# Other constants in the table of durations that orders the queues of a hybrid DeltaNet and window-attention layer

## The chip, the cores and the metric

The kernel runs on one core of one Trainium2 chip. The core has five instruction queues that matter here: TensorE (PE, its weight loads shown as PEld), VectorE (DVE), ScalarE (ACT), GpSimd (POOL) and SyncE (SP), which only issues DMAs. Each queue runs its instructions strictly in order; an instruction that waits holds up everything behind it on its queue. The metric is the device time of one execution, in microseconds. Before the change it is 1352.76 us, the median of three runs (1352.02 to 1355.77).

## The reference

One encoder layer: RMSNorm, one input projection, two groups of heads that read the same normalised rows, one output projection, and a residual. All is float32, with 2048 rows and a model width of 1024.

```python
h = rms_norm(x, norm_w[l])
proj = h @ w_in[l]
# A: 4 DeltaNet heads of 128, chunks of 64, forward and backward
qkv = jax.nn.silu(centred_depthwise_conv(concat([q, k, v]), conv_w))
t_inv = triangular_solve(eye + m, eye, lower=True, unit_diagonal=True)
u = t_inv @ (v * beta); w = t_inv @ (k * beta * exp(g))
# scan over chunks:
v_new = u_i - w_i @ state
o     = (q_i * exp(g_i)) @ state + a_i @ v_new
state = state * exp(g_last) + k_dec.T @ v_new
# B: 8 query heads of 64 over 2 key heads, |i-j| <= 128, a sink logit per head
p = exp(scores - mx); out = (p / (sum(p) + exp(sink - mx))) @ v
mix = concat([rms_norm(dn, w) * silu(dn_z), sw * silu(sw_z)])
x = x + mix @ w_out[l]
```

## The kernel before

**Two stages.** The function `phase_a` (up to some 800 us) splits the normalised x into a high and a low part (type float32r) and makes every product of the projection out of three matmuls of 512 columns: `proj_feat` (L186 to L188, tiles `pf_c` and `pf_z`, transposed results) and `proj_seq` (L197 to L199, `pq_q`). `conv_pair` (L212 to L246) takes a pair of channel blocks: it has ScalarE write the first tap into `acc` (L233) and VectorE add the four others straight from the PSUM tile `pf_c` (L237), and stores q and k into `kq_d`, v into `v_d`. A bank of `pf_c` comes free when the last L237 on it is done. `attend` treats one block of 128 query rows: scores `s` (L339 and L340), masked row maxima on VectorE (L341, one custom instruction per head, which writes `pr`), the exponentials on ScalarE (L346), the scaling of `pr` on GpSimd (L355), transposes of `pr` on TensorE (L360, `pt`), their split (L364 and L365, `ph` and `pl`) and the products with v.

**The DeltaNet stage.** `phase_b` has for each of four heads: `pre_front` (from L588), `pre_back` (from L671) and `scan` (from L750). `pre_front` runs over four groups of four chunks, in the order 1, 2, 0, 3: it loads `kq` (L604, 512 KB, two buffers) and `vt`, transposes them (L621 `tr`, L660 `trv`), forms the Gram matrices `gh` (L641), has VectorE scale them into `ma` (L650) and stores these to `m_d` in DRAM (L655). `pre_back` loads `L` from `m_d` and solves all chunks' triangular systems at once by 31 steps of two VectorE instructions each (L687 into `tm`, L691 into `X`), stores X (L692), loads it in spread form (`xc`, L740) and completes the inverse with 16 times four small matmuls (L703, `pza`, `pra`, `pzb`, `prb`). `scan` goes over 16 chunks in both directions: `pk` (L767), `r` on VectorE (L769), `py` (L776), `yk` and `y` on ScalarE (L781, L783), `po` (L778, L785, L794), the new state `S` on VectorE (L788) and the sums into `oacc` (L801 to L805). `post_rows` transposes `oacc` (L833, `tro`), loads the gate `zt` (L835), multiplies (L836) and stores to `mix_dn`. `out_half` is the output projection: its window-attention half (`pcs`) stands in the program behind the first `pre_front`, its DeltaNet half (`pcd`, L559 to L561, with loads L550 and L556 and the sum L562) at the end. Names carry the head, the direction or the group, and the chunk: `ma3_2_0` is head 3, group 2, direction 0.

**What sets the order.** The program is written head after head, but the queues aren't run in that order. `set_order` (from L875) takes all instructions, builds the graph of what must come before what (data, buffers that have to come free, PSUM banks), and gives each a duration from a table, `cost` (L1003), and each edge a lag: `LAG` between engines, `SAME` for a result that its own engine reads, and for a DMA the issue time (`cost` for SP) plus a time to land (`LAG["SP"]`, `move`, which is bytes / 300 and also occupies one common bus, and `late`). `plan` is a list scheduler: it picks for the engine that is free earliest the ready instruction of the highest rank. It is run forwards and backwards twelve times, each pass ranking by the times of the one before, and the order with the least end by its own reckoning is kept. The result is pinned: each instruction gets a dependency on its predecessor on its queue. So the table decides nothing but the order; no instruction, tile or buffer hangs on it.

Of the kernel before, what the change touches and what calls it, by code (L numbers as in the profile page):

```python
# [13 lines left out]
DRAM = bass.MemoryType.DRAM  # L14
# [860 lines left out]
def set_order(tc):  # L875
# [127 lines left out]
    def cost(i, eng):  # L1003
        o = aps(i.outs)
        m, ins = size(o[0]), aps(i.ins)
        if eng == "SP":
            return 500
        if eng == "PE":
            if i.is_transpose:
                return 110  # L1010
            if "float32r" in str(i.ins[0].dtype):
                return max(112, m / 2.4 + 14)
            return 2 * (max(m, size(ins[1]) if len(ins) > 1 else P, 40) / 1.2 + 5)
        scalars = sum(size(a) == 1 for a in ins)
        if eng == "Activation":
            return 60 + 0.86 * m + 85 * (scalars > 0) + 110 * (len(o) > 1)
        m = max([m] + [size(a) for a in ins])
        if eng == "DVE":
            if i.opcode == "Reciprocal":
                return 70 + 6.2 * m  # L1020
            if i.opcode == "TensorScalarPtr" and len(ins) - scalars < 2:
                return 60 + 0.6 * m
            return 70 + 1.04 * m + 55 * (scalars > 0) + 10 * (i.opcode == "ISA")
        if i.opcode == "TensorTensor":
            return 350 + 165 * min(m, 4) if m <= 16 else 180 + 2.1 * m
        return 150 + 1.02 * m

    total = len(succ)
    dur = [cost(i, e) for i, e in insts] + [0] * (total - n)
# [3 lines left out]
    for k in range(total):  # L1033
        if eng[k] == "SP":
            a = aps(insts[k][0].outs)[0]
            move[k] = a.ap[0][1] * size(a) * 4 / 300
            spread = [x.ap[0][0] == 0 for x in aps(insts[k][0].ins)]
# [178 lines left out]
```

## Time and profile before

| | before |
|---|---|
| median of 3 runs | 1352.76 us |
| the profiled execution, device time | 1354.61 us |
| its span in the trace | 1352.8 us |
| mean granted TensorE clock | 0.982 |
| GpSimd busy | 442.8 us |
| ScalarE busy | 684.2 us |
| transfers | 217.99 MB at a mean of 161 GB/s |

A profile is one execution. Its page gives the busy time of each engine, the span cut into slices, the transfers, the chain of work that ended last (followed back from the last instruction, at each step to what released it) and the costliest groups of instructions. A row of a group reads: line, engine, operation, out <- in by tile names, shape, count | busy us, mean ns of one | idle time of the engine ahead of them, and what ended most of it. A row of waits reads: engine, tile and line that waited <- what released it: us in all, number of waits, the longest. A row of the timeline reads: start, duration, engine, line, operation, tiles, and in brackets the idle time ahead of it and what ended it. Since matmuls overlap, a matmul's duration is longer than its share of the queue; starts tell how fast a row of them runs.

### The profile page before, as it was taken

How to read it: one execution, taken by the hardware profiler on the slowest of the kernel's cores; microseconds unless marked ns; L12 is line 12 of the kernel's file. 1: busy time of each engine (PE TensorE's matmuls, PEld its weight loads, DVE VectorE, ACT ScalarE, POOL GpSimd, SP SyncE). 2: the span in 40 equal slices, each digit the busy share in tenths (PEclk: the TensorE clock that was granted, in tenths of full speed). 3: DMA queues.
4: the chain of work that ended last, by engine and by line, in shares of the span. 5: the costliest groups of instructions: out<-in, count | busy, mean ns of one | idle time of the engine just before them, and what ended most of it. 6: DMA issues, size and time to landing. Idle time of an engine off the chain costs nothing.

```text
span 1352.8 us, 22281 instructions
## 1 busy us (share of the span) xinstructions
PE 1252.7 (93%) x7034; PEld 1052.7 (78%) x7034; DVE 938.7 (69%) x2362; ACT 684.2 (51%) x2009; POOL 442.8 (33%) x574
## 2 busy tenths in 40 slices
PE   5999989999999999999999997887898998997988
PEld 5998868888898987876788776776686786785766
DVE  4422577767878778888979767777779779755333
ACT  6321354425767777866645326664465644454200
POOL 2330062104666677864412114212521510300000
PEclk9999999999999999998999998997999999998999
DMA  8342254244522344412267537788786874646575
GB/s 282 113 135 94 72 161 156 74 129 137 176 74 87 118 143 121 148 32 79 95 223 215 175 113 231 223 230 250 231 245 182 251 189 146 192 129 195 165 247 187
DMA packets 238261, 217.99 MB, mean 161 GB/s; under 512 B 50368, under 2 KB 189376, under 8 KB 238144
## 3 DMA queue, kind: packets, MB, share of 16 engines
q1 hardware_dynamic: 238144, 216.58, 52.8%
q8 instruction: 56, 0.92, 0.3%
q14 instruction: 61, 0.50, 0.1%
HBM read 143.05 MB, written 73.47 MB: 160 GB/s over the span
## 4 chain that ended last, share of the span: by engine, by line
PE 63%; DVE 14%; DMA 9%; ACT 5%; POOL 4%; issue 4%; SPq 1%; POOLq 0%; DVEq 0%; ACTq 0%
PE pf_c L186 4%; PE pf_c L188 4%; PE pf_c L187 4%; PE pf_z L186 4%; PE pf_z L188 4%; PE pf_z L187 3%; PE pt L360 2%; PE pcd L560 2%; PE pcd L559 2%; DMA m_d<-ma 2%; PE pcd L561 2%; DVE acc L237 2%; DMA kq<-kq_d 2%; PE pq_q L197 2%; PE pq_q L199 2%
## 5 line engine op out<-in xcount | busy, mean ns | idle before, releaser
L186 PE MATMUL pf_c<-xhi,wh_c 128*128 128x512 f32 x384 | 151.2, 405 | 4.2 <-DVE acc L237 4.2
L237 DVE SCALAR_TENSOR_TENSOR acc<-pf_c,cw,acc 128x512 f32<-128x512 f32 (+1 forms) x192 | 140.0, 744 | 21.6 <-ACT acc L233 19.8
L187 PE MATMUL pf_c<-xlo,wh_c 128*128 128x512 f32 x384 | 149.8, 401 | 0.0
L188 PE MATMUL pf_c<-xhi,wl_c 128*128 128x512 f32 x384 | 149.4, 402 | 0.0
L355 POOL TENSOR_SCALAR pr<-pr,st 128x384 f32<-128x384 f32 (+1 forms) x128 | 85.3, 684 | 79.6 <-DVE st L353 38.4
L186 PE MATMUL pf_z<-xhi,wh_z 128*128 128x512 f32 x256 | 92.5, 404 | 1.4 <-DVE zo L210 1.4
L781 ACT ACTIVATE yk<-py,ck 128x128 f32<-128x128 f32 x120 | 43.9, 366 | 93.5 <-PE py L776 92.7
L187 PE MATMUL pf_z<-xlo,wh_z 128*128 128x512 f32 x256 | 91.0, 398 | 0.0
L188 PE MATMUL pf_z<-xhi,wl_z 128*128 128x512 f32 x256 | 90.7, 398 | 0.0
L346 ACT ACTIVATE pr<-pr,st 128x384 f32<-128x384 f32 (+1 forms) x128 | 76.3, 598 | 23.4 <-DVE st L345 21.3
L186 PEld LDWEIGHTS pf_c<-xhi,wh_c 128*128 128x128 f32 x384 | 73.0, 191 | 19.2 <-DVE acc L237 4.5
L188 PEld LDWEIGHTS pf_c<-xhi,wl_c 128*128 128x128 f32 x384 | 72.9, 190 | 15.7 <-issue 0.4
L187 PEld LDWEIGHTS pf_c<-xlo,wh_c 128*128 128x128 f32 x384 | 73.1, 190 | 14.2
L360 PE MATMUL pt<-ident,pr 128*128 128x128 f32 x368 | 73.3, 281 | 7.5 <-POOL pr L355 3.9
L341 DVE CUSTOM_DVE_ANT_0 pr<-s,mask,sink 128x384 f32<-128x384 f32 (+1 forms) x128 | 72.8, 593 | 10.1 <-PE s L340 4.7
L365 DVE TENSOR_TENSOR pl<-pt,ph 128x512 fp32r<-128x512 f32 x92 | 62.1, 683 | 20.6 <-ACT ph L364 16.8
L364 ACT ACTIVATE ph<-pt 128x512 fp32r<-128x512 f32 x92 | 53.6, 596 | 44.5 <-PE pt L360 38.3
L360 PEld LDWEIGHTS pt<-ident,pr 128*128 128x128 f32 x368 | 46.9, 142 | 26.6 <-POOL pr L355 10.6
L197 PE MATMUL pq_q<-wh_q,xhi 128*128 128x256 f32 x256 | 66.6, 287 | 0.1
L198 PE MATMUL pq_q<-wh_q,xlo 128*128 128x256 f32 x256 | 66.1, 285 | 0.0
L199 PE MATMUL pq_q<-wl_q,xhi 128*128 128x256 f32 x256 | 65.5, 286 | 0.0
L559 PE MATMUL pcs<-wohs,mhs 128*128 128x512 f32 x128 | 58.0, 453 | 7.6 <-ACT wohs L541 3.9
(250 smaller groups left out, 3668.2 us busy)
## 6 DMA issues: line engine op xcount, KB each, us to landing
m_d<-ma SPq DMA_DIRECT2D x32, 512.0 KB, 5.9
kqc<-kq_d SPq DMA_DIRECT2D x120, 128.0 KB, 3.4
ws_c<-wt SPq DMA_DIRECT2D x48, 256.0 KB, 3.7
xr<-x SPq DMA_DIRECT2D x16, 512.0 KB, 5.4
ws_z<-wt SPq DMA_DIRECT2D x32, 256.0 KB, 3.8
kq<-kq_d SPq DMA_DIRECT2D x16, 512.0 KB, 6.3
at<-m_d SPq DMA_DIRECT2D x128, 64.0 KB, 3.2
xrs<-x SPq DMA_DIRECT2D x32, 256.0 KB, 3.7
```

Source lines behind the costliest of these rows:

```text
L186: T.matmul(ps, hi[:, k, cs], xhi[b][:, k], start=(k == 0), stop=False)
L187: T.matmul(ps, hi[:, k, cs], xlo[b][:, k], start=False, stop=False)
L188: T.matmul(ps, lo[:, k, cs], xhi[b][:, k], start=False, stop=(k == KC - 1))
L197: T.matmul(ps[:, :n], xh, hi[:, k, :n], start=(k == 0), stop=False)
L198: T.matmul(ps[:, :n], xl, hi[:, k, :n], start=False, stop=False)
L199: T.matmul(ps[:, :n], xh, lo[:, k, :n], start=False, stop=(k == KC - 1))
L237: V.scalar_tensor_tensor(av, ps[:, lo:], cw[:, i, k : k + 1], av, ALU.mult, ALU.add)
L341: V.tensor_tensor_reduce(pr[j][:, :n], ps[:, :n], mask[:, lo * P : hi * P], 1.0, sink[:, hh : hh + 1], ALU.add, ALU.max, accum_out=mx[:, j ...
L346: A.activation(pr[j][:, :n], pr[j][:, :n], AF.Exp, bias=nm[:, j : j + 1], accum_out=den[:, j : j + 1])
L355: G.tensor_scalar(pr[j][:, :n], pr[j][:, :n], den[:, j : j + 1], 1.0, ALU.mult, ALU.mult)
L360: T.transpose(pt[:, j], pr[j][:, (kb - lo) * P : (kb - lo + 1) * P], ident)
L559: T.matmul(ps, mh[:, k], wh[:, k, ns], start=(k == 0), stop=False)
```

## The change

The table gets other constants, in four parts. For SP, the general lag of 2400 ns goes, an issue costs 520 or 670 ns instead of 500 (by the number of dimensions of its access pattern), and a new function `landing` gives each transfer its time to land: by size, with 1900 ns and 190 bytes per ns for loads, 1800 ns for what is written to DRAM at 450 or 190 bytes per ns, 1000 ns more for loads that read one row for many partitions and 1200 ns more for runs of under 64 elements. `move`, the common bus, stays. For TensorE, VectorE and ScalarE the fixed part of each duration grows by 3 to some 20 ns for most forms; operands that begin at a partition other than 0 get 115 ns more on VectorE and ScalarE (`off`). For GpSimd the fixed part grows by 60 to 70 ns. Nothing else in the kernel is changed.

```diff
-LAG = {"PE": 205, "DVE": 140, "Activation": 160, "Pool": 120, "SP": 2400}
+LAG = {"PE": 205, "DVE": 140, "Activation": 160, "Pool": 120, "SP": 0}
...
-            return 500
+            dims = max(sum(c > 1 for _, c in list(a.ap)[1:]) for a in (o[0], ins[0]))
+            return 520 if dims < 2 else 670
+        off = 115 * (o[0].ap[0][0] > 0 and o[0].offset // o[0].ap[0][0] % P > 0)
...
-                return max(112, m / 2.4 + 14)
+                return max(112, m / 2.4 + 18) + 5
...
-            return 70 + 1.04 * m + 55 * (scalars > 0) + 10 * (i.opcode == "ISA")
+            return 88 + 1.04 * m + 55 * (scalars > 0) + 10 * (i.opcode == "ISA") + off
...
-        return 150 + 1.02 * m
+        return 210 + 1.02 * m + 0.4 * off
+
+    def landing(i):
+        o, a = aps(i.outs)[0], aps(i.ins)[0]
+        n = o.ap[0][1] * size(o) * 4
+        if o.tensor.name in tiles and "DRAM" in str(tiles[o.tensor.name].space):
+            return 1800 + n / (450 if sum(c > 1 for _, c in o.ap) < 3 else 190)
+        run = min([c for t, c in list(a.ap) + list(o.ap) if t == 1] or [1])
+        return 1900 + n / 190 + 1000 * any(t == 0 for t, _ in a.ap) + 1200 * (run < 64)
...
-            late[k] = 2000 * any(spread)
-        lag = LAG[eng[k]] + move[k] + late[k] if k < n else 0
+            late[k] = landing(insts[k][0])
+        lag = LAG[eng[k]] + late[k] if k < n else 0
```

The orders of all five queues come out otherwise, with the same instructions in them. Three places:

On VectorE, in the first stage, where the first attention block's softmax (`pr0`, `st0`) meets the first convolutions (`acc4` and `acc5`, which empty the banks `pf_c`), stood before:

```order
L345 TENSOR_SCALAR st0_0_1496<-st0_0_1496 128x1
L349 TENSOR_TENSOR st0_0_1496<-sink_140,st0_0_1496 128x4
L341 ISA pr0_1_0_1562,st0_1_1566<-s0_4_1567,mask_130,sink_140 128x256
L341 ISA st0_1_1566 128x1
L281 TENSOR_TENSOR t1k3_1807<-t1k3_1807,rsk3_1813 128x128
L341 ISA pr0_1_1_1563,st0_1_1566<-s0_5_1573,mask_130,sink_140 128x256
L341 ISA st0_1_1566 128x1
L345 TENSOR_SCALAR st0_1_1566<-st0_1_1566 128x1
L237 SCALAR_TENSOR_TENSOR acc4_0_2046<-pf_c4_0_0_2050,cw_128,acc4_0_2046 128x512
L237 SCALAR_TENSOR_TENSOR acc5_0_2048<-pf_c5_0_0_2080,cw_128,acc5_0_2048 128x512
L237 SCALAR_TENSOR_TENSOR acc4_0_2046<-pf_c4_0_0_2050,cw_128,acc4_0_2046 128x512
L237 SCALAR_TENSOR_TENSOR acc5_0_2048<-pf_c5_0_0_2080,cw_128,acc5_0_2048 128x512
```

and now, from the rotary step `t1q1` on:

```order
L281 TENSOR_TENSOR t1q1_1460<-t1q1_1460,rsq1_1466 128x512
L300 TENSOR_TENSOR kd2_1445<-t1k2_1433,kd2_1445 128x2x128
L237 SCALAR_TENSOR_TENSOR acc4_0_2046<-pf_c4_0_0_2050,cw_128,acc4_0_2046 128x512
L237 SCALAR_TENSOR_TENSOR acc5_0_2048<-pf_c5_0_0_2080,cw_128,acc5_0_2048 128x512
L237 SCALAR_TENSOR_TENSOR acc4_0_2046<-pf_c4_0_0_2050,cw_128,acc4_0_2046 128x512
L237 SCALAR_TENSOR_TENSOR acc5_0_2048<-pf_c5_0_0_2080,cw_128,acc5_0_2048 128x512
L237 SCALAR_TENSOR_TENSOR acc4_0_2046<-pf_c4_0_0_2050,cw_128,acc4_0_2046 128x511
L237 SCALAR_TENSOR_TENSOR acc5_0_2048<-pf_c5_0_0_2080,cw_128,acc5_0_2048 128x511
L237 SCALAR_TENSOR_TENSOR acc4_0_2046<-pf_c4_0_0_2050,cw_128,acc4_0_2046 128x510
L237 SCALAR_TENSOR_TENSOR acc5_0_2048<-pf_c5_0_0_2080,cw_128,acc5_0_2048 128x510
L237 SCALAR_TENSOR_TENSOR acc4_0_2046<-pf_c4_0_1_2110,cw_128,acc4_0_2046 128x512
L178 TENSOR_TENSOR wl_c8_0_2412<-ws_c8_0_6_2425,wh_c8_0_2411 128x2x256
```

The eight L237 rows of the first bank pair, and the first of the next bank, have moved from behind the softmax rows of the heads 0 to 5 to a place ahead of all of them; the first L341 row (`pr0_0_0`) now stands two rows behind this piece.

On TensorE, in the DeltaNet stage, at head 2's `pre_front`, where the Gram matmuls `gh2_1_1` and `gh2_2_0` read `kq` of the groups 1 and 2 and `tr2_0_0` is the first to read the reloaded buffer of group 0, stood before:

```order
L641 MATMUL gh2_1_1_11260<-kq2_1_11205 128x256 x2
L794 MATMUL po0_0_12_10664<-y0_0_12_10669,at0_0_12_10655 128x128
L621 MATMUL tr2_2_1_11312<-ident_66,kq2_2_11285 128x128 x4
L776 MATMUL py0_1_12_10685<-r0_1_12_10683,tt0_0_9626 128x128
L767 MATMUL pk0_0_13_10749<-S0_0_12_10672,kqc0_0_13_10747 128x128
L660 MATMUL trv2_2_11355<-ident_66,vt2_2_11287 128x128 x4
L785 MATMUL po0_1_12_10686<-yk0_1_12_10689,ks0_0_8737 128x128
L833 MATMUL tro0_1_10723<-ident_66,oacc0_1_10321 128x128 x4
L641 MATMUL gh2_2_0_11329<-kq2_2_11285 128x256 x2
L621 MATMUL tr2_0_0_11377<-ident_66,kq2_0_11365 128x128 x4
```

and now, from the same first row, the first part of what lies between:

```order
L641 MATMUL gh2_1_1_11260<-kq2_1_11205 128x256 x2
L621 MATMUL tr2_2_1_11312<-ident_66,kq2_2_11285 128x128 x4
L778 MATMUL po0_0_12_10664<-S0_0_11_10628,kqc0_0_12_10657 128x128
L785 MATMUL po0_0_12_10664<-yk0_0_12_10667,ks0_3_8807 128x128
L778 MATMUL po0_1_12_10686<-S0_1_11_10650,kqc0_1_12_10679 128x128
L559 MATMUL pcs2_0_8986<-wohs_8867,mhs2_8980 128x512
L660 MATMUL trv2_2_11355<-ident_66,vt2_2_11287 128x128 x3
L794 MATMUL po0_0_12_10664<-y0_0_12_10669,at0_0_12_10655 128x128
L660 MATMUL trv2_2_11355<-ident_66,vt2_2_11287 128x128
L641 MATMUL gh2_2_0_11329<-kq2_2_11285 128x256 x2
L833 MATMUL tro0_1_10723<-ident_66,oacc0_1_10321 128x128
L560 MATMUL pcs2_0_8986<-wohs_8867,mls2_8979 128x512
```

Behind this piece follow two more rows of `tro0_1` and ten of the chunk product `pcs2_0`, and only then `tr2_0_0`. Twelve matmuls of `pcs2_0`, each 512 columns wide, now stand between `gh2_1_1` and `tr2_0_0`, and some scan rows (`py0_1_12`, `pk0_0_13`) have gone from there.

On VectorE, in the same stage, where head 2's solve (`tm2`, `X2`) runs beside head 1's scan (`r1`, `S1`, `oacc1`), the end of the solve and the first rows behind it read before:

```order
L691 TENSOR_TENSOR X2_12303<-X2_12303,tm2_30_12398 128x31
L769 SCALAR_TENSOR_TENSOR r1_1_12_12071<-pk1_1_12_12069,negc_5022,vs1_0_10052 128x128
L788 SCALAR_TENSOR_TENSOR S1_0_12_12060<-S1_0_11_12016,egt_5024,po1_0_12_12052 128x128
L632 RECIPROCAL ssk3_12586<-ssk3_12586 128x4
L633 TENSOR_TENSOR bp3_12588<-beta_4996,ssk3_12586 128x2x4
L804 SCALAR_TENSOR_TENSOR oacc1_3_11555<-po1_0_12_12052,egc_5026,oacc1_3_11555 128x128
L822 SCALAR_TENSOR_TENSOR sso1_1_12087<-sso1_1_12087 128x8
L562 TENSOR_TENSOR xrs8_0_9218<-xrs8_0_9218,pcs8_0_9220 128x512
L805 TENSOR_TENSOR oacc1_3_11555<-po1_0_12_12052,oacc1_3_11555 128x128
L650 SCALAR_TENSOR_TENSOR ma3_2_0_12680<-gh3_2_0_12717,bp3_12588,dc3_2_0_12677 128x256
L650 SCALAR_TENSOR_TENSOR ma3_2_1_12684<-gh3_2_0_12717,bp3_12588,dc3_2_1_12681 128x256
L650 SCALAR_TENSOR_TENSOR ma3_2_0_12680<-gh3_2_0_12717,bp3_12588,dc3_2_0_12677 128x256
```

and now, in the middle of the solve:

```order
L687 TENSOR_TENSOR tm2_11_12341<-L2_12302,X2_12303 128x240
L802 TENSOR_TENSOR oacc1_1_11709<-po1_0_7_11832,oacc1_1_11709 128x128
L691 TENSOR_TENSOR X2_12303<-X2_12303,tm2_11_12341 128x20x12
L788 SCALAR_TENSOR_TENSOR S1_1_7_11862<-S1_1_6_11818,egt_5024,po1_1_7_11854 128x128
L687 TENSOR_TENSOR tm2_12_12344<-L2_12302,X2_12303 128x247
L650 SCALAR_TENSOR_TENSOR ma3_2_0_12680<-gh3_2_0_12717,bp3_12588,dc3_2_0_12677 128x256
L691 TENSOR_TENSOR X2_12303<-X2_12303,tm2_12_12344 128x19x13
L769 SCALAR_TENSOR_TENSOR r1_1_8_11895<-pk1_1_8_11893,negc_5022,vs1_1_9892 128x128
L687 TENSOR_TENSOR tm2_13_12347<-L2_12302,X2_12303 128x252
```

The eight L650 rows of head 3's group 2 (`ma3_2`) stood behind the last solve step and now stand singly between its steps, from the twelfth on.

More of the change, by code (lines that the diff above doesn't have):

```diff
@@ L1019, in cost @@
             if i.opcode == "Reciprocal":
[L1020 removed]
+                return 80 + 6.2 * m
             if i.opcode == "TensorScalarPtr" and len(ins) - scalars < 2:
[L1022 to L1023 removed]
+                return 70 + 0.6 * m
+            return 88 + 1.04 * m + 55 * (scalars > 0) + 10 * (i.opcode == "ISA") + off
         if i.opcode == "TensorTensor":
[L1025 to L1026 removed]
+            return 420 + 165 * min(m, 4) if m <= 16 else 250 + 2.1 * m
+        return 210 + 1.02 * m + 0.4 * off
[6 more added lines that the diff above has]
+        return 1900 + n / 190 + 1000 * any(t == 0 for t, _ in a.ap) + 1200 * (run < 64)
     total = len(succ)
```

7 lines of the change are left out of this document (3 added, 4 removed).

## The prediction

> **What bounds the kernel now.** I read the page first, for the shares and for where TensorE is not full, and then the same stretch by stage.
>
> ```profile
> PE 1252.7 (93%) x7034; PEld 1052.7 (78%) x7034; DVE 938.7 (69%) x2362; ACT 684.2 (51%) x2009; POOL 442.8 (33%) x574
> ...
> PE 63%; DVE 14%; DMA 9%; ACT 5%; POOL 4%; issue 4%; SPq 1%; POOLq 0%; DVEq 0%; ACTq 0%
> ```
>
> TensorE is busy for 93% of the span and makes 63% of the chain that ended last; the other 37% of the chain are places where it stood and another engine or a transfer was late. No instruction is added or removed, so the change can only move those places. The windows (columns: stretch, length, then the busy time of PE, PEld, DVE, ACT and POOL, the granted clock, the DMA share, GB/s) tell where they are:
>
> ```profile
> 700.00:800.00 100.00, 98.46 (x440) 79.58 (x439) 81.65 (x165) 37.89 (x108) 15.34 (x15) 1.00 0.59 177
> 800.00:900.00 100.00, 82.38 (x521) 71.03 (x520) 66.93 (x179) 58.62 (x218) 30.88 (x24) 0.95 0.77 215
> 900.00:1000.00 100.00, 85.06 (x461) 70.05 (x462) 71.84 (x207) 53.48 (x224) 36.27 (x27) 0.90 0.80 240
> 1000.00:1100.00 100.00, 91.75 (x611) 77.81 (x610) 86.57 (x269) 58.34 (x241) 29.03 (x22) 1.00 0.72 211
> 1100.00:1200.00 100.00, 91.23 (x608) 77.92 (x607) 75.24 (x235) 44.86 (x162) 14.44 (x10) 1.00 0.60 168
> 1200.00:1300.00 100.00, 87.86 (x462) 71.29 (x461) 49.06 (x129) 34.63 (x121) 3.27 (x2) 0.97 0.59 185
> ```
>
> Up to 800 us TensorE is almost full. From 800 to 1300 it idles 61.7 us (the sum of 100 minus its busy time), and between 800 and 1000 its clock falls as well. That second stage, the DeltaNet heads, is where an order can win or lose most. How fast TensorE gets through a row of matmuls is read from starts, since its busy times overlap:
>
> ```profile
> 220.10 0.40 PE L186 MATMUL pf_c<-xhi,wh_c 128*128 128x512 f32 x1
> 220.34 0.39 PE L187 MATMUL pf_c<-xlo,wh_c 128*128 128x512 f32 x1
> ```
>
> and, for the 128-wide float32 ones,
>
> ```profile
> 1111.51 0.39 PE L767 MATMUL pk<-S,kqc 128*128 128x128 f32 x2
> 1111.73 0.39 PE L778 MATMUL po<-S,kqc 128*128 128x128 f32 x2
> ```
>
> A 512-wide matmul starts 0.24 us after the one before it (0.23 over a longer row), a 128-wide float32 one 0.22 us.
>
> **The change, place by place.** The new constants raise most engine durations by a few per cent alike, TensorE and VectorE by 3 to 4% on the 512-wide shapes, which by itself leaves an order as it is. What differs is GpSimd (60 to 70 ns more per operation) and the DMAs: a 512 KB load from a feature tensor is now taken to land later (1900 + 524288/190 = 4.7 us instead of 2400 + 524288/300 = 4.1), small loads and all stores sooner. I take the places where TensorE waited longest and look whether the new order changes what stands there.
>
> Place A, the first convolutions beside the first softmax:
>
> ```profile
> PE pf_c L186 <- DVE acc L237: 4.2, 1, 4.2
> ```
>
> What VectorE did just then, and the window around it:
>
> ```profile
> 177.35 1.22 DVE L281 TENSOR_TENSOR t1q<-t1q,rsq 128x512 f32<-128x512 f32 x1 [1.20 <-POOL rsq L280]
> 178.50 0.47 DVE L341 CUSTOM_DVE_ANT_0 pr<-s,mask,sink 128x256 f32<-128x256 f32 x1
> 183.04 6.00 DVE L237 SCALAR_TENSOR_TENSOR acc<-pf_c,cw,acc 128x512 f32<-128x512 f32 x9
> ...
> 180.00:200.00 20.00, 15.66 (x70) 12.56 (x69) 16.06 (x41) 12.15 (x30) 10.62 (x20) 0.91 0.30 103
> ```
>
> TensorE stood 4.2 us for a PSUM bank that the accumulations of L237 had to empty, and these began at 183.04, behind 4.5 us of softmax rows that began at 178.50. In the new VectorE order the nine accumulations come right behind t1q and one kd row, so they end about 4.1 us earlier (4.5 less some 0.4 for kd). TensorE itself reaches the bank about 1.9 us sooner, because twelve score matmuls and four transposes are moved behind it (an estimate from the rows: twelve at about 0.12, four at 0.11). What is left of the wait is 4.2 - 4.1 + 1.9 = 2.0 us, so 2.2 us go. The granted clock in the 20 us around it is 0.91, a loss of 1.8 us of array time right behind the wait; I count that as gone too. A is **-4.0 us**; bounds 0 and -6.0 (the whole wait and the clock). What is late next is the first softmax, which TensorE now asks for 15 us of matmuls later.
>
> Place B, the reload of kq (both buffers of the tag are in use, so the third load waits until the Gram matmuls of L641 have read the first):
>
> ```profile
> PE tr L621 <- DMA kq<-kq_d: 2.4, 3, 1.1
> ```
>
> The load's median time to land (last number), the window around the waits, and single rows with the wait ahead of them in brackets:
>
> ```profile
> kq<-kq_d SPq DMA_DIRECT2D x16, 512.0 KB, 6.3
> ```
>
> ```profile
> 910.00:945.00 35.00, 26.78 (x122) 21.05 (x122) 26.82 (x78) 17.83 (x85) 8.44 (x7) 0.76 0.80 242
> ```
>
> ```profile
> 918.23 1.09 PE L621 MATMUL tr<-ident,kq 128*128 128x128 f32 x4 [1.14 <-DMA kq<-kq_d]
> ...
> 933.75 0.49 PE L776 MATMUL py<-r,tt 128*128 128x128 f32 x2 [1.65 <-DVE r L769]
> ...
> 937.86 0.90 PE L621 MATMUL tr<-ident,kq 128*128 128x128 f32 x3 [0.96 <-DMA kq<-kq_d]
> ```
>
> For head 2 the order puts twelve more 512-wide matmuls (12 x 0.23 = 2.8 us) between the last Gram matmul on the old buffer and the first transpose on the new one for group 0, and for group 3 24 more of them and 15 more float32 ones (5.5 + 3.3 = 8.8 us). The two waits of 1.14 and 0.96 us are covered: -2.1 us. In this stretch the clock is 0.76 over 35 us, 8.4 us of array time, while TensorE waited there some 6.7 us in seven places, the longest single one 1.65. kq has 2.1 of the 6.7, so I give it the same share of the clock, 2.6 us. Bounds of that part: 0 and 8.4.
>
> The Trainium skill ("TensorE: Matmul & The Clock Gate", Part 1, the HAM clock gate) states that the array drops to half clock only after an idle window of about 3.4 us. By that rule waits of 1 us cost no clock and B would be -2.1 instead of -4.7. The trace does not agree here: the clock is 0.76 where no single wait passes 1.65 us. Only in place A, with 4.2 us, do the two agree.
>
> For head 1 the same two distances shrink: four float32 matmuls fewer before group 0 (0.9 us), five fewer before group 3 (1.1). Landing takes 6.3 us there as well, so I charge both: +2.0 us (bounds 0 and +2.0). B together: **-2.7 us**.
>
> Place C, the solves. Each head's 62-step triangular solve (L687 and L691) is a chain on VectorE, between the store of m_d and the matmuls of L703; its buffers come free only when the former head's solve is done, so the heads' solves follow each other. VectorE in the solves of heads 1 and 2, all of its work:
>
> ```profile
> 897.75:947.55 49.80, 39.20 (x131) 0.83 0.82 247
> 1008.90:1043.64 34.74, 33.33 (x123) 1.00 0.65 195
> ```
>
> the solve's own in head 2's, and two groups of rows that are moved:
>
> ```profile
> 1008.90:1043.64 34.74, 22.48 (x62) 1.00 0.65 195
> ```
>
> ```profile
> L650 DVE SCALAR_TENSOR_TENSOR ma<-gh,bp,dc 128x256 f32<-128x256 f32 x128 | 56.2, 476 | 9.1 <-DMA m_d<-ma 5.3 <-PE gh L641 3.1
> L804 DVE SCALAR_TENSOR_TENSOR oacc<-po,egc,oacc 128x128 f32<-128x128 f32 x64 | 21.8, 343 | 8.1 <-PE po L794 7.9
> ```
>
> In head 2's solve VectorE is full (33.3 of 34.7 us), so a row put between its steps costs its whole time. The new order puts eight rows of L650 there (8 x 0.476 = 3.8 us) and takes out some seven small ones of 0.3 us and a net nothing of larger ones: about +1.8 us. In head 3's solve two S rows, one each of L804 and L805 and a 512-wide zt row leave: about -2.0 us. Head 1's solve has VectorE idle for 10.6 of 49.8 us, in the stretch of place B: it waits for TensorE's rows, so what B frees there is not held back by the solve. C is **-0.2 us**, bounds +1.8 and -2.0.
>
> Place D, the end of the last scan:
>
> ```profile
> PE po L778 <- DVE zt L836: 4.9, 2, 4.6
> ```
>
> The issues of SP that go before it:
>
> ```profile
> 1237.02 1.70 SPq L556 DMA_DIRECT2D xrd<-part  x2
> ...
> 1238.77 0.42 SPq L835 DMA_DIRECT2D zt<-zdn  x1
> ```
>
> TensorE stands 4.6 us because zt, ahead of the scan's S row on VectorE, waits for its load. That order is unchanged on VectorE. SP now issues one of the two xrd loads behind the zt load instead of ahead of it: **-0.8 us** (half of 1.70), bound 0, because the load also waits for the store from the same buffer. The out projection that follows has the same pattern in both.
>
> ```profile
> span 1352.8 us, 22281 instructions
> ```
>
> Sum: -4.0 - 2.7 - 0.2 - 0.8 = -7.7 us. The profiled execution took 1354.61 us (span 1352.8 and 1.8 around it), so this gives 1346.9 for such a run. It lies 1.85 above the median of 1352.76; on the median the sum gives 1345.06, and I forecast **1345.0 us**.
>
> **The rivals.** First: the gains go into the next wait. From 800 to 1200 us each head's solve, scan and the next solve hang on each other, and a wait taken out at one place lets TensorE run into the next late producer. For it speaks that 37% of the chain lies outside TensorE; against it that place A lies in a stage where TensorE is nearly full, so that its 4 us stay won unless the attention waits longer. Time: 1352.8.
>
> Second, on the other side: **the attention runs ahead of GpSimd**. From the twelfth to the fourteenth block the new TensorE order has 26 convolution matmuls fewer ahead of the transposes of pr (26 x 0.23 = 6.0 us), with the same GpSimd work ahead of the scaling L355 that these need.
>
> ```profile
> PE pt L360 <- POOL pr L355: 3.9, 8, 1.0
> ...
> 620.00:645.00 25.00, 22.88 (x99) 16.56 (x100) 21.80 (x57) 13.69 (x36) 10.20 (x14) 0.86 0.29 85
> ```
>
> If GpSimd cannot be 6.0 us earlier, TensorE waits those 6.0 us once, and another window of low clock like that at 620 to 645 (0.14 x 25 = 3.5 us of array time, taken half, 1.7) comes with it: 7.7 us. It decides from the point at which GpSimd's idle time ahead of L355 is under 6 us; in this stretch GpSimd is busy for 10.2 of 25 us, which speaks against it, but what it idles for is VectorE's softmax rows, and VectorE is busy for 21.8 of 25, which speaks for it. With the gains of A to D absorbed as in the first rival this gives 1352.8 + 7.7 = 1360.5 us. That the change does nothing is excluded: the orders differ on every engine.
>
> A third, better than the forecast: with the waits of 910 to 945 thinned, its whole clock loss goes (8.4 instead of 2.6) and head 1's reloads stay hidden (2.0 not paid): 1345.0 - 7.8 = 1337.2 us.
>
> **How the numbers follow.** Forecast case 0.45, with a range of its own of 1339 to 1350; gains absorbed 0.21; GpSimd late 0.24; clock loss gone 0.10. The measurement of this kernel can tell about 0.3% (4.1 us) from no change, so "within" is 1348.7 to 1356.8. Faster: 0.10 and all of the forecast case but 0.05, 0.50. Within: 0.05, and the absorbed case less a little at its upper edge, 0.25. Slower: 0.25. The low end takes all lower bounds, -6.0 - 10.5 - 2.0 - 0.8 = -19.3, so 1333; the high end is the second rival with head 2's +1.8, 1362.
>
> **What would show it.** A: the wait of pf_c for acc falls under 2.5 us and the clock at 180 to 200 rises to about 1. B: waits of tr for kq between 900 and 950 vanish, new ones of about 1 us stand near 815 to 840, and the clock from 900 to 1000 rises above 0.93. C: head 2's solve is about 2 us longer, head 3's 2 us shorter. D: a wait of about 4 us for zt is still there. I am wrong if TensorE's idle time before 700 us grows, above all for pr (second rival), or if the stage from 800 to 1200 keeps its length with the waits only renamed (first).

## The result, and the profile after

| kernel | median, us | runs | ratio to before on the same chip, 95% interval |
|---|---|---|---|
| before | 1353.23 | 20 | |
| after | 1344.58 | 20 | 0.9942 (0.9927 to 0.9956) |
| after, second measurement (after_again) | 1343.80 | 6 | 0.9927 (0.9905 to 0.9948) |

The kernel became 0.6 to 0.7% faster. The forecast was 1345.0 us, the median is 1344.58. The sum was right; its terms mostly were not, as the rest of this document shows. One execution of the run nodma below took 3076.81 us at a granted clock of 1.00 and is left out of its ratio.

The profiled execution of after took 1352.23 us, the longest of its 20 runs (1338.69 to 1352.23). Its page:

```profile
span 1350.5 us, 22285 instructions
...
PE 1252.5 (93%) x7034; PEld 1058.7 (78%) x7034; DVE 946.0 (70%) x2362; ACT 685.2 (51%) x2009; POOL 445.4 (33%) x574
```

The busy times are those of before to within 0.8%, as they must be with the same instructions. The places the prediction named, and 760 to 780 us, as windows of after (stretch, length, busy PE, PEld, DVE, ACT, POOL, granted clock, DMA share, GB/s):

```profile
180.00:200.00 20.00, 16.88 (x75) 13.70 (x74) 17.39 (x32) 11.56 (x25) 9.20 (x16) 0.91 0.41 134
620.00:645.00 25.00, 23.91 (x129) 19.72 (x128) 24.21 (x66) 16.71 (x43) 10.55 (x14) 1.00 0.21 65
760.00:780.00 20.00, 17.48 (x70) 13.74 (x70) 14.41 (x38) 3.26 (x12) 0.00 (x0) 0.91 0.58 167
910.00:945.00 35.00, 29.25 (x137) 22.98 (x138) 27.75 (x81) 15.17 (x58) 9.05 (x8) 0.85 0.73 214
```

Place A (180 to 200) still has the low clock. At place B (910 to 945) it is 0.85, where before had 0.76. And at 620 to 645, where the prediction saw nothing to win, the clock is now full and TensorE is busy for 23.91 of 25 us: before had 22.88 us and 0.86 there. Of TensorE's waits in the attention stage, 300 to 700 us, this is the second largest of before (behind the 3.9 us for `pr` that the prediction shows):

```profile
PE pt L360 <- DVE pl L365: 3.0, 4, 1.1
```

and these are the three largest of after:

```profile
PE pt L360 <- POOL pr L355: 1.7, 3, 1.1
PE po L367 <- DVE ot L374: 1.4, 1, 1.4
PE pt L360 <- DVE pl L365: 1.4, 3, 0.6
```

The softmax that the second rival expected to come too late is late less often. The start of the attention's last transpose (674.7 and 665.7 us in these rows) tells the same, before and then after:

```profile
L360 PE MATMUL pt<-ident,pr x368: 270/272/477, 217.5 to 674.7; 128*128 128x128 f32 x184
```

```profile
L360 PE MATMUL pt<-ident,pr x368: 270/272/332, 233.9 to 665.7; 128*128 128x128 f32 x184
```

The last transpose of the attention starts 9.0 us earlier, although the first starts 16 us later.

The second stage is best read by its solves, since each head's 31 steps (L691) are easy to find and each solve waits for the former one's buffers. Heads 2 and 3 of before, and the same of after_again:

```profile
L691 DVE TENSOR_TENSOR X<-X,tm x31: 180/353/1179, 1009.5 to 1043.5; 128x31 f32<-128x31 f32 x2, 128x60 f32<-128x60 f32 x2, 128x87 f32<-128x87 f32 x2, 128x112 f32<-128x112 f32 x2
...
L691 DVE TENSOR_TENSOR X<-X,tm x31: 184/348/419, 1112.2 to 1146.6; 128x31 f32<-128x31 f32 x2, 128x60 f32<-128x60 f32 x2, 128x87 f32<-128x87 f32 x2, 128x112 f32<-128x112 f32 x2
```

```profile
L691 DVE TENSOR_TENSOR X<-X,tm x31: 181/364/1198, 1001.2 to 1037.6; 128x31 f32<-128x31 f32 x2, 128x60 f32<-128x60 f32 x2, 128x87 f32<-128x87 f32 x2, 128x112 f32<-128x112 f32 x2
...
L691 DVE TENSOR_TENSOR X<-X,tm x31: 191/350/422, 1103.7 to 1136.1; 128x31 f32<-128x31 f32 x2, 128x60 f32<-128x60 f32 x2, 128x87 f32<-128x87 f32 x2, 128x112 f32<-128x112 f32 x2
```

From the start of its first L691 step to that of its last, head 2's solve takes 36.4 us instead of 34.0, head 3's 32.4 instead of 34.4. With the same rows of the other heads and of the experiments below, the execution falls into six pieces. Each column gives the pieces of one profile in us; X0 is the start of the last L691 step of head 0's solve, and so on:

| piece | before | m_place | m_att | m_first | after | after_again | m_second | zo_first | best |
|---|---|---|---|---|---|---|---|---|---|
| start to last L360 | 674.7 | 677.0 | 671.3 | 666.6 | 665.7 | 665.3 | 674.7 | 664.3 | 663.7 |
| to X0 | 121.3 | 120.0 | 126.9 | 126.0 | 127.4 | 123.3 | 122.7 | 123.8 | 124.2 |
| X0 to X1 | 151.4 | 152.6 | 148.5 | 147.2 | 147.0 | 147.4 | 146.0 | 141.6 | 142.8 |
| X1 to X2 | 96.1 | 95.7 | 95.4 | 97.1 | 104.2 | 101.6 | 100.9 | 104.8 | 104.5 |
| X2 to X3 | 103.1 | 103.5 | 103.1 | 103.6 | 96.7 | 98.5 | 96.1 | 98.1 | 96.9 |
| X3 to the end | 206.2 | 206.5 | 206.7 | 207.6 | 209.5 | 207.1 | 207.4 | 206.3 | 206.8 |

The first four have before's order behind X0, the last five that of after. b_kq below, before's order with twelve matmuls moved, has 674.6, 123.0, 153.3, 93.8, 106.6 and 208.1. The pieces X1 to X2 and X2 to X3 repeat within some 4 us for one order, and differ by 6 to 7 us between the orders, with opposite signs. X0 to X1 repeats less well: 147.2 to 153.3 in before's order, 141.6 to 147.4 in that of after.

### The profile page after: what moved, and what is told of

Read it like the earlier page. It is cut to its first block, busy times and chain, and to the rows that moved or that the text cites. A ratio compares the mean times of both kernels' runs of the same rounds, so it can differ in the third digit from the quotient of the medians.

```text
span 1350.5 us, 22285 instructions
## 1 busy us (share of the span) xinstructions
PE 1252.5 (93%) x7034; PEld 1058.7 (78%) x7034; DVE 946.0 (70%) x2362; ACT 685.2 (51%) x2009; POOL 445.4 (33%) x574
## 4 chain that ended last, share of the span: by engine, by line
PE 34%; DMA 10%; DVE 8%; ACT 4%; POOL 2%; issue 2%; SPq 1%; DVEq 0%; POOLq 0%; ACTq 0%
PE pf_c L188 2%; DMA dc<-gr_d 2%; PE pf_c L186 2%; PE pf_c L187 2%; PE pcd L560 2%; PE pcd L559 2%; PE pcd L561 2%; PE pcs L559 1%; PE po L785 1%; PE py L776 1%; PE pcs L560 1%; DMA m_d<-ma 1%; PE pcs L561 1%; PE po L794 1%; PE pk L767 1%
## 5 line engine op out<-in xcount | busy, mean ns | idle before, releaser
L237 DVE SCALAR_TENSOR_TENSOR acc<-pf_c,cw,acc 128x512 f32<-128x512 f32 (+2 forms) x192 | 138.9, 744 | 24.1 <-ACT acc L233 20.9
L355 POOL TENSOR_SCALAR pr<-pr,st 128x384 f32<-128x384 f32 (+1 forms) x128 | 85.1, 682 | 55.4 <-DVE st L353 45.5
L346 ACT ACTIVATE pr<-pr,st 128x384 f32<-128x384 f32 (+1 forms) x128 | 76.2, 597 | 16.8 <-DVE st L345 15.6
L341 DVE CUSTOM_DVE_ANT_0 pr<-s,mask,sink 128x384 f32<-128x384 f32 (+1 forms) x128 | 72.3, 593 | 5.1 <-PE pt L360 3.3
L360 PE MATMUL pt<-ident,pr 128*128 128x128 f32 x368 | 71.2, 274 | 3.3 <-POOL pr L355 1.7
L650 DVE SCALAR_TENSOR_TENSOR ma<-gh,bp,dc 128x256 f32<-128x256 f32 x128 | 56.3, 474 | 15.5 <-PE gh L641 10.3
L360 PEld LDWEIGHTS pt<-ident,pr 128*128 128x128 f32 x368 | 47.7, 140 | 18.8 <-POOL pr L355 5.4
L233 ACT ACTIVATE acc<-pf_c,cw 128x512 f32<-128x512 f32 x48 | 32.4, 682 | 58.0 <-PE pf_c L188 56.3
L769 DVE SCALAR_TENSOR_TENSOR r<-pk,negc,vs 128x128 f32<-128x128 f32 x120 | 41.3, 344 | 27.0 <-PE pk L767 26.2
```

The lines of the kernel that those rows point to most:

```text
L237: V.scalar_tensor_tensor(av, ps[:, lo:], cw[:, i, k : k + 1], av, ALU.mult, ALU.add)
L341: V.tensor_tensor_reduce(pr[j][:, :n], ps[:, :n], mask[:, lo * P : hi * P], 1.0, sink[:, hh : hh + 1], ALU.add, ALU.max, accum_out=mx[:, j ...
L346: A.activation(pr[j][:, :n], pr[j][:, :n], AF.Exp, bias=nm[:, j : j + 1], accum_out=den[:, j : j + 1])
L355: G.tensor_scalar(pr[j][:, :n], pr[j][:, :n], den[:, j : j + 1], 1.0, ALU.mult, ALU.mult)
L360: T.transpose(pt[:, j], pr[j][:, (kb - lo) * P : (kb - lo + 1) * P], ident)
L650: V.scalar_tensor_tensor(mas[d][:, c], gh[:, k], bp[:, d, cc : cc + 1], gms[d][:, c : c + 1].to_broadcast([P, 2, P]), ALU.mult, ALU.mult,)
```

## The experiments

**Where in the program the gain lies.** Both orders are planned, and each instruction takes its planned time from one of the two, by the stretch it lies in. The queues are sorted by these times, so that each stretch has one kernel's order unchanged, except at the start, as m_place will show (cuts of the code are marked by dots):

```diff
+def mixed(one, two, takes):
...
+    base = [sorted(b[k] for k in queue["PE"]) for b in (b1, b2)]
+    b2 = np.interp(b2, base[1], base[0])
+    key = [float(b2[k]) if takes(b1[k]) else b1[k] for k in range(len(b1))]
+    for k in topo:
+        for s, _ in nxt[k]:
+            key[s] = max(key[s], key[k] + 0.01)
+    return {e: sorted(q, key=lambda k: (key[k], k)) for e, q in queue.items()}
...
+    pin(tc, one[0], mixed(one, two, lambda b: b < 740e3))              # m_first
+    pin(tc, one[0], mixed(one, two, lambda b: b >= 740e3))             # m_second
+    pin(tc, one[0], mixed(one, two, lambda b: b < 270e3))              # m_place
+    pin(tc, one[0], mixed(one, two, lambda b: 270e3 <= b < 740e3))     # m_att
```

> The order of after up to about 765 us of the trace (projection, convolutions, attention), the order of before behind it. Theory of the prediction: the first stage holds only place A, so 4.0 us less than before, about 1349; the rest of the gain needs the second stage. Rival from the trace of after: all of the gain lies in the first stage, in the attention from 300 to 700 us, and the second stage gives some of it back: 8 us less or more, 1345 or below.

> The order of before up to about 765 us, the order of after behind it. Theory of the prediction: places B, C and D, 3.7 us less than before, about 1349.5. Rival from the trace: no gain, between 0 and 6 us slower than before, 1353 to 1359.

> The order of after up to about 275 us only (the start and place A), the order of before behind it. Theory of the prediction: place A alone, 4.0 us less than before, about 1349. Rival from the trace: the start loses 3 us and place A wins 2 of them back, so 1 to 2 us slower than before, about 1354.5.

> The order of after only from about 275 to 765 us (the attention blocks, with the convolutions and gates between them), the order of before ahead of and behind it. Theory of the prediction: nothing was costed here, so 0, about 1353; its second rival would make it 7.7 us slower, 1361. Rival from the trace: the whole gain sits here, 8 to 11 us less than before, 1342 to 1345, with fewer waits of pt (L360) for pr and pl and no half clock near 631 us.

| kernel | median, us | ratio, 95% interval |
|---|---|---|
| before, on this chip | 1351.18 | |
| m_first | 1349.31 | 0.9982 (0.9965 to 0.9999) |
| m_second | 1349.67 | 0.9986 (0.9968 to 1.0004) |
| m_place | 1354.23 | 1.0020 (1.0000 to 1.0041) |
| m_att | 1359.32 | 1.0061 (1.0039 to 1.0082) |

m_place is 2.7 us slower (0.20% of 1351.18) where the prediction's theory had 4.0 us of gain. But its start is not that of after. These are the first 100 us of before, after and m_place, then the first issue of SP and the first matmul in after and in m_place:

```profile
0.00:100.00 100.00, 85.96 (x641) 82.70 (x642) 37.46 (x60) 40.50 (x89) 30.38 (x61) 1.00 0.57 178
0.00:100.00 100.00, 84.93 (x627) 81.99 (x628) 35.91 (x60) 41.05 (x89) 30.06 (x60) 1.00 0.55 171
0.00:100.00 100.00, 81.54 (x623) 79.70 (x624) 34.88 (x57) 39.74 (x87) 28.15 (x56) 1.00 0.54 171
```

```profile
0.72 0.40 SPq L105 DMA_DIRECT2D xr<-x  x1
...
8.03 1.97 PE L127 MATMUL xt<-ident,xr 128*128 128x128 f32 x8 [8.03 <-DVE xr L123]
```

```profile
0.72 0.39 SPq L42 DMA_DIRECT2D ident<-ident  x1
...
12.09 1.97 PE L127 MATMUL xt<-ident,xr 128*128 128x128 f32 x8 [12.09 <-DVE xr L123]
```

`np.interp` gives all that after plans ahead of its first matmul one and the same time, and SP then takes those loads as the program lists them: the constants first, the rows of x as the sixth. So TensorE begins 4.1 us late in m_place, and in m_first too (12.14 us), which neither before nor after does. How much of that is left at the end was not measured; m_place alone therefore does not settle place A, and the gain of m_first may be too small by part of it. The start of after itself loses less: TensorE starts 641 matmuls in the first 100 us of before, 627 in after, 629 in after_again and 633 in zo_first, which at 0.23 us each is some 2 to 3 us.

m_att is a miss for both theories. Where the two orders meet, TensorE waits for L237; the waits of m_att at 255 to 300 us:

```profile
PE pf_c L186 <- DVE acc L237: 6.4, 2, 4.0
```

This seam is dear, but its attention nevertheless ends 3.4 us earlier than before's. The profile is the fastest of m_att's eight executions (1353.70 us), so where the 8.1 us of its median go is not shown. In time, the medians bear out neither theory of the halves. That m_first and m_second took about the 1349 and 1349.5 us of the prediction's theory is chance, since before took only 1351.18 on this chip: each half gives 0.14 to 0.18%, together 0.32%, while the whole gives 0.58%. The intervals are 0.15 to 0.2% wide to each side, and the late start of m_first accounts for up to 0.3% (4.1 us), so nothing here shows that the halves need each other.

**Which constants carry it.**

```diff
+    insts, _, _, _, queue = plan_with(tc, ("SP",))                                # only_dma
...
+    insts, _, _, _, queue = plan_with(tc, ("PE", "DVE", "Activation", "Pool"))    # nodma
...
+        return cost(i, e) * (1 + 0.03 * random.Random(kind).uniform(-1, 1))       # rand1, rand2: before's table
```

> Before with the new constants of SP alone (issue, landing), the durations of all engines as before. Its TensorE order lies close to that of after (5 places off in the mean, 15 from before). Theory that the transfers' landing times carry the change: the time of after, ratio about 0.994. Rival of the prediction's reading, in which places A and B come of the durations as well: between, about 0.997.

> Before with the new durations of the four computing engines, the transfers as before. If the landing times carry the change and the rest adds nothing: ratio 0.998 to 1.002. If the new durations work on their own as well as the landing times do: about 0.996.

> Before with every duration of the table multiplied by a factor drawn from 0.97 to 1.03, one for each kind of instruction (engine, operation and size); landing times as before. Theory that truer constants make the better order: no gain, ratio 0.998 to 1.005. Rival, that each new table is a draw from a spread of orders some 5 us wide to both sides: a gain or a loss of several us with no truer number in the table.

> As rand1 with another draw of the factors (0.97 to 1.03 for each kind of instruction). If such errors of the table cost time as a rule: slower than before by 0.5 per cent or more again. If rand1 was an unlucky draw from a spread around before: as often below 1 as above, within 0.5 per cent.

| kernel | median, us | ratio, 95% interval |
|---|---|---|
| only_dma | 1343.31 | 0.9955 (0.9935 to 0.9975) |
| nodma | 1358.49 | 1.0043 (1.0026 to 1.0061) |
| rand1 | 1371.39 | 1.0166 (1.0142 to 1.0190) |
| rand2 | 1359.79 | 1.0049 (1.0023 to 1.0074) |

The constants of SP (issue and landing times) bring most of the gain alone, 0.45% of the 0.58 to 0.73%, though the interval of only_dma holds both of its expectations (0.994 and about 0.997); the new durations of the engines alone make the kernel slower, which neither expectation of nodma had. So the GpSimd constants are not needed for the gain. Random errors of up to 3% in the table cost 1.7% in rand1, more than either of its expectations had, and 0.5% in rand2. The two tables with the new constants of SP are faster than before, and the three others are slower. That is few: orders from slightly different tables lie over 2% apart here, and that the gain comes of truer landing times, and is not a lucky draw among such orders, is not shown. Nor does an earlier end of the attention suffice: its last transpose starts at 663.8 us in only_dma, but also at 670.4 in nodma and 671.3 in rand2, ahead of before's 674.7, and both kernels are slower than before.

One thing, though, is no merit of any constant. The window of 600 to 700 us, first before, m_second, m_place and b_kq (told of next), all with before's attention, then after, nodma, rand1 and rand2:

```profile
600.00:700.00 100.00, 96.44 (x468) 75.22 (x467) 89.63 (x222) 60.07 (x154) 38.50 (x49) 0.97 0.36 114
600.00:700.00 100.00, 96.24 (x470) 75.04 (x469) 90.04 (x222) 60.69 (x154) 38.51 (x49) 0.98 0.36 115
600.00:700.00 100.00, 96.24 (x471) 75.18 (x470) 90.20 (x223) 61.84 (x154) 39.64 (x51) 0.98 0.34 109
600.00:700.00 100.00, 96.51 (x469) 75.41 (x468) 89.81 (x223) 60.09 (x154) 38.52 (x49) 0.97 0.36 114
```

```profile
600.00:700.00 100.00, 98.27 (x493) 80.06 (x492) 86.26 (x209) 59.98 (x157) 33.52 (x46) 1.00 0.41 131
600.00:700.00 100.00, 97.05 (x484) 77.00 (x483) 90.24 (x226) 63.04 (x164) 38.82 (x52) 1.00 0.38 123
600.00:700.00 100.00, 97.87 (x495) 77.83 (x494) 94.50 (x238) 65.94 (x155) 43.68 (x57) 1.00 0.29 88
600.00:700.00 100.00, 98.09 (x492) 78.47 (x491) 94.14 (x231) 65.03 (x168) 39.48 (x54) 1.00 0.38 119
```

Before's order has a lower clock here (0.97 or 0.98) in each of its four profiles, and every other order, the random ones too, has 1.00. Two to three us of clock (0.02 to 0.03 of 100) were a bad spot of that one order.

**Single waits.** In b_kq the twelve matmuls of `pcs3_0` stand ahead of the first transposes of head 2's reloaded `kq`, in before's order:

```diff
 L641 MATMUL gh2_2_0<-kq2_2 128x256 x2
-L621 MATMUL tr2_0_0<-ident,kq2_0 128x128 x4
-L621 MATMUL tr2_0_1<-ident,kq2_0 128x128 x2
 L559 MATMUL pcs3_0<-wohs,mhs3 128x512
...
 L561 MATMUL pcs3_0<-wols,mhs3 128x512
+L621 MATMUL tr2_0_0<-ident,kq2_0 128x128 x4
+L621 MATMUL tr2_0_1<-ident,kq2_0 128x128 x2
```

> The order of before with one thing moved: the twelve matmuls of pcs3_0 stand ahead of tr2_0_0 (six transposes) on TensorE, so that the reload of kq of head 2, group 0, has 2.8 us more. Theory of the prediction: the wait of 1.14 us goes, and about half of the 2.6 us of clock that place B was given: 1.1 to 2.4 us less than before, ratio 0.998 to 0.999. Rival: by the milestones of the traces the solves set the pace there; the wait goes, but the solve of head 1 ends when it did, and the time is that of before.

Measured: 1354.94 us, ratio 1.0031 (1.0010 to 1.0051). Its waits of TensorE from 900 to 980 us, and the window of place B:

```profile
PE pcs L559 <- DVE xrs L562: 4.3, 5, 1.6
...
PE po L778 <- DVE oacc L805: 2.2, 1, 2.2
...
PE tr L621 <- DMA kq<-kq_d: 0.3, 1, 0.3
```

```profile
910.00:945.00 35.00, 27.41 (x135) 21.72 (x133) 28.87 (x78) 18.91 (x84) 9.05 (x8) 0.85 0.79 248
```

Of the wait for `kq`, 0.3 us is left (before had 2.4 us from 900 to 980), and the clock is 0.85 instead of 0.76. But the waits for the sums of the other product (L562) and for L805 have grown, and TensorE's work in the 35 us is 27.41 instead of 26.78 us. Head 1's solve lasts 49.2 us as it did (49.3). So the wait was not what this solve hung on. Why the kernel is even slower was not found; by its profile, the longest of its twelve executions, the loss does not lie here, since that solve, which runs beside this place, begins 3.6 us behind before's (901.7 and 898.1) and ends 3.5 behind (950.9 and 947.4).

In zo_first, in after's order, the gate rows stand ahead of a weight split that waits for its load (ScalarE's queue):

```diff
 L243 ACTIVATE th11_1<-acc11_1 128x1026
-L177 ACTIVATE wh_z14_1<-ws_z14_1_4 128x2x256
 L209 ACTIVATE zo12_1_0<-pf_z12_1_0 128x512
 L209 ACTIVATE zo12_1_0<-pf_z13_1_0 128x512
+L177 ACTIVATE wh_z14_1<-ws_z14_1_4 128x2x256
```

(on VectorE one L210 row likewise ahead of the split L178, the other ahead of L682). The reason lies in after's profile, the SP queue, then ScalarE, then TensorE:

```profile
754.21 0.62 SPq L680 DMA_DIRECT2D L<-m_d  x1
754.88 1.44 SPq L681 DMA_DIRECT2D X<-eye  x1
756.43 0.60 SPq L679 DMA_DIRECT2D L<-m_d  x1
757.08 4.14 SPq L176 DMA_DIRECT2D ws_z<-wt  x1
761.32 0.41 SPq L246 DMA_DIRECT2D v_d<-acc  x1
761.84 0.37 SPq L176 DMA_DIRECT2D ws_z<-wt  x1
```

```profile
764.33 0.63 ACT L177 ACTIVATE wh_z<-ws_z 128x512 fp32r<-128x512 f32 x1 [5.95 <-DMA ws_z<-wt]
764.87 0.58 ACT L209 ACTIVATE zo<-pf_z 128x512 f32<-128x512 f32 x1
```

```profile
766.45 0.50 PE L186 MATMUL pf_z<-xhi,wh_z 128*128 128x512 f32 x1 [2.52 <-DVE zo L210]
```

The weight load `ws_z` stands on SP behind the solve's loads of `m_d`, ScalarE waits 5.95 us for it with the gate `zo` queued behind, and TensorE waits 2.52 us for the bank that `zo` holds.

> The order of after with one thing moved: the two gate rows zo12_1_0 stand ahead of the weight split of ws_z14_1_4 on ScalarE (L209 ahead of L177) and ahead of L682 and the split on VectorE, so that the bank of pf_z no longer hangs on a weight load that SP holds back behind the solve's loads of m_d. Theory that the attention's gain is partly given back at this wait: the wait of pf_z (2.5 us) and the low clock of 760 to 780 us go, up to 4 us less than after, ratio to before about 0.991. Rival: the first solve, which hangs on the loads of m_d and not on TensorE, sets the start of the DeltaNet stage; the last gate products end earlier but pza of head 0 waits as much longer, the end of the first solve stays at about 793 us, and the time is that of after, ratio 0.994.

Measured: 1341.43 us, ratio 0.9947 (0.9927 to 0.9967), that is, the time of after. The wait fell from 2.5 to 0.6 us; the window of zo_first, and the same of after_again, where nothing was moved:

```profile
760.00:780.00 20.00, 19.43 (x86) 15.17 (x84) 18.63 (x47) 4.75 (x15) 0.00 (x0) 1.00 0.46 137
```

```profile
760.00:780.00 20.00, 20.00 (x88) 15.74 (x87) 17.96 (x46) 5.05 (x15) 0.00 (x0) 1.00 0.47 147
```

The second execution of after has no such wait at all, with `ws_z` behind the same loads on SP. So the wait does not come in every execution of this order, and its 2.5 us were no reserve that zo_first could win. It is not a thing of one execution either: it is 3.8 us in m_first, 5.0 in m_att, 1.4 in before and 2.1 in b_kq. What decides its length is not shown. The rival was right on the time and wrong in one point: head 0's solve did not stay at 793 us, it ended at 788 in zo_first and in after_again alike.

**After once more, and a combination.** best takes before's order up to about 100 us, after's behind it, and zo_first's rows:

```diff
+    insts, queue = one[0], mixed(one, two, lambda b: b >= 100e3)
+    hop(insts, queue, "Activation", ("zo12_1_0", "pf_z12_1_0"), ("wh_z14_1", "ws_z14_1_4"), True)
...
```

> The order of after, once more, for its profile and for its time on the same chip as the others. All theories: ratio 0.994 to 0.996. By the milestones of the other profiles its first solve ends 3 us or more ahead of before's, and the second stage from there to the end has the length of m_second's, some 550 us.

> The order of before up to about 100 us, that of after behind it, and the gate rows moved as in zo_first. If the 2 to 4 us that the start of after loses in its profiles and the 3 us of the handover both count: ratio 0.989 to 0.991, ahead of after. If what is won ahead of the first solve is taken back by the waits between the solves: as after, 0.994.

after_again: ratio 0.9927 (0.9905 to 0.9948), somewhat under the expected 0.994 to 0.996. Head 0's solve ended 7.4 us ahead of before's, the rest lasted 554.6 us (556.8 before, some 550 expected). best: 1340.24 us, ratio 0.9911 (0.9890 to 0.9932), the lowest of all kernels. It lies 3.6 us under after_again on the same chip, at the upper edge of what was expected, but the intervals overlap: better than before is shown, better than after is not.

## Why the prediction was right, and where it was not

The forecast came out: 1345.0 us against 1344.58. The means of the pieces give the account as it was: 9.6 us won up to the end of the attention (674.7 in before, m_second and b_kq; 665.1 in after, after_again and zo_first), 2.5 lost from there to X0 (122.3 to 124.8, the same profiles), 4.9 won to X1 (149.9 to 145.0, from here on the table's four and five columns), 7.1 lost to X2 (96.1 to 103.2), 6.0 won to X3 (103.3 to 97.3), 0.6 lost at the end. The first of these and the two that cancel stand clear of the scatter; the others hardly or not. That is 10.3 us in the profiles, where the runs give 7.9 (0.58% of 1353) and 9.9 (0.73%). By halves, 7.1 us were won up to X0, where the prediction had the 4.0 of place A, and 3.2 behind it, where B, C and D gave 3.7: the sizes are near, but they come about in another way.

**Place A (-4.0): about zero.** The step that failed is "so they end about 4.1 us earlier". It is seen best in the run best, which has before's start and after's place A. Its rows on VectorE, ScalarE, then TensorE:

```profile
175.88 1.23 DVE L281 TENSOR_TENSOR t1q<-t1q,rsq 128x512 f32<-128x512 f32 x1
178.90 0.43 DVE L300 TENSOR_TENSOR kd<-t1k,kd 128x256 fp32r<-128x256 f32 x1 [1.78 <-ACT kd L299]
180.02 6.01 DVE L237 SCALAR_TENSOR_TENSOR acc<-pf_c,cw,acc 128x512 f32<-128x512 f32 x9 [0.70 <-ACT acc L233]
```

```profile
178.44 0.42 ACT L299 ACTIVATE kd<-t1k 128x256 fp32r<-128x256 f32 x1 [1.34 <-PE ptq L322]
178.77 0.58 ACT L323 ACTIVATE q<-ptq 128x512 fp32r<-128x512 f32 x1
179.25 1.84 ACT L233 ACTIVATE acc<-pf_c,cw 128x512 f32<-128x512 f32 x3
```

```profile
184.77 0.50 PE L186 MATMUL pf_c<-xhi,wh_c 128*128 128x512 f32 x1 [3.12 <-DVE acc L237]
```

The nine rows begin 3.0 us earlier (180.02, before 183.04), not 4.1: VectorE now idles 2.5 us for ScalarE, whose first taps (L233) stand behind a row that waits for TensorE. I had moved one engine's queue and left its supplier out. TensorE comes to the bank 1.9 us sooner (181.65 instead of 183.6), as estimated, so 4.2 - 3.0 + 1.9 = 3.1 us of wait stay, the measured 3.12. The 1.1 us won go again at 237 us, where a later bank waits 1.2 us. The 1.8 us of clock did not come back in after (0.91). And a term was missing altogether: the start, where after loses the 2 to 3 us that its matmul counts show.

**The attention (not costed; second rival +7.7): about -12.** This is where the gain is, and the prediction looked at it only for a loss: 9.6 us at its end, after the 2 to 3 us lost at the start. It counted that TensorE's transposes come 6.0 us of matmuls earlier, but not that the rows of the softmax on VectorE, ScalarE and GpSimd move forward with them: the last L341, L346 and L355 start 9.6, 10.0 and 9.7 us earlier in after. GpSimd did not come too late: the waits for `pr` fell from 3.9 to 1.7 us. From 300 to 700 us TensorE idles for 6.9 us instead of 11.0, and two to three us are the low clock of before's order near 631 us. Where the other half of the 12 us lies was not traced.

**Place B (-2.7): the waits moved as foreseen, the time did not follow.** In the five profiles with after's order none of these waits for `kq` is left from 890 to 945 us (one of 0.4 to 1.2 us stands later, at 978 to 987, in four of them). But b_kq took one of them away singly and nothing came of it, and head 1's solve, which runs beside this place, takes 46.2 to 49.9 us in after's order and 47.1 to 49.3 in before's. So a wait of TensorE in a stretch where the solve, the scan and the product of the other half wait for each other was no term of a sum here. The share of the clock (2.6 us) had two faults. The nine waits of TensorE from 910 to 945 us add up to 8.1 us, not 6.7, which would have made it 2.2. And the 0.76 did not belong to the order: m_first, m_att and m_place, with before's order there, have 0.80, 0.85 and 1.00. The charge for head 1 (2.0 us) appears in part: from 805 to 845 us TensorE waits for `kq` for 0.3 us in after and best, 1.3 in after_again, 2.5 in zo_first and 3.4 in m_second, and not at all in before. The prediction did not see a new wait of 2.1 to 2.7 us in all five, for `kqc`; both kinds in after_again:

```profile
833.40 0.66 PE L621 MATMUL tr<-ident,kq 128*128 128x128 f32 x4 [1.27 <-DMA kq<-kq_d]
884.93 0.46 PE L767 MATMUL pk<-S,kqc 128*128 128x128 f32 x2 [2.15 <-DMA kqc<-kq_d]
```

Something else shortened X0 to X1 in spite of it, and did so ahead of the start of head 1's solve: that lies 94.6 to 97.5 us behind X0 with after's order and 99.4 to 105.5 with before's. What it was, was not tried singly.

**Place C (-0.2): right, in signs and nearly in sizes.** Head 2's solve: +1.8 foreseen, 2.4 to 3.3 longer measured (34.0 to 36.4, 36.8 and 37.3). Head 3's: -2.0 foreseen, 2.0 to 2.8 shorter (34.4 to 32.4 and 31.6). Where VectorE was full (33.3 of 34.7 us), a row put between cost its time. But these two belong to larger shifts, +7.1 and -6.0 us of the pieces that hold them, which no step had; they cancel too.

**Place D (-0.8): right in sign, and without effect on the piece.** The wait for zt in the last scan, after, from 1200 to 1300 us:

```profile
PE po L778 <- DVE zt L836: 3.2, 1, 3.2
```

It is 4.6 to 4.8 us in the four profiles with before's order there, and 3.2, 2.4, 4.8, 2.3 and 4.0 in the five with that of after (after, after_again, m_second, zo_first, best): 1.3 us less in the mean. The piece from X3 to the end is no shorter for it (206.8 and 207.4).

**The rivals.** The first (gains go into the next wait) is seen at place A and b_kq. The second went the other way. The third had the clock of place B come back whole: it is 0.85 in after, 0.90 in after_again and 1.00 in best, for one order there. So the agreement of 1345.0 with 1344.58 is luck for the most part: a missed gain of 12 us and a missed loss of 2 to 3 at the start stand against gains of 4.0 at place A and 4.7 at place B that did not come as described. It bears out the sign and little more.

## What to carry to other kernels

When an order changes, take a milestone that repeats (here the end of each solve) and compare pieces between milestones, in several profiles: three of the four pieces behind X0 agreed within some 4 us for one order, and X0 to X1 within 6, where whole executions of after spread over 13.5 us. When two orders are spliced for a test, look at the splice and at the start in the trace before the time is read. Before a wait is booked as gain, follow the supplier of the waiting engine on its own queue as well, since the row ahead of which something was moved may wait for a third engine. In this kernel the constants of the transfers mattered more than the durations of the engines. And an order can hold a bad spot that other orders lack, so a few deliberately disturbed tables help to tell a better table from a better draw; two, as here, are too few to decide it.

## What the runs showed of the hardware

- The order alone did not set the clock. Place A has the same wait of 3.1 us in after, best and zo_first; the clock there is 0.91 in the first two and 1.00 in zo_first:

```profile
180.00:200.00 20.00, 16.88 (x79) 13.71 (x79) 18.51 (x33) 12.30 (x25) 10.01 (x18) 1.00 0.40 140
```

  The Trainium skill ("TensorE: Matmul & The Clock Gate", Part 1) says that the window in which activity is counted is free-running, so that the number of slow matmuls at a kernel's start differs between runs of one kernel. These rows, in the middle of a kernel, agree with a window that is not tied to the order. Yet before's spot near 631 us came in all four of its profiles (0.86 to 0.93 from 620 to 645 us).
- Executions of one kernel spread by some 0.5% to each side of the median (after: 1338.69 to 1352.23 us), with mean clocks of 0.978 to 0.987. A single profile can therefore be 7.7 us off the median, as after's was.
- An issue of a DMA on SP took 4.14 us right behind the two loads of `m_d` for the solve and the load of X, where another of the same kind soon after took 0.37. It did so in each profile with this order there: 3.87 us in after_again, 3.95 in zo_first and 3.80 in best.
